# Late 1 / rms in both FFNs' first pairs, the second SSM group's gate and norm behind head 1, and whole first operands of out_proj, in a hybrid decoder layer

## The chip, the cores and the metric

The kernel runs on one core of one Trainium2 chip, as a single launch. The metric is device time in microseconds (us), taken as the median of several runs; lower is better. One execution was also recorded by the hardware profiler, and all rows of the trace come from it. The engines are named as in the profile: PE is the matrix engine (PEld its weight loads), DVE the vector engine, ACT the scalar engine, POOL GpSimd, SP the engine that issues nearly all DMAs.

## What is computed

One layer of a decoder that runs two mixers side by side, over 1048 tokens of width 1024: 16 learned meta tokens, 1024 prompt tokens and 8 single-token samples with states of their own.

```python
h = h + 0.5 * swiglu(rmsnorm(h, n1), w1g, w1u, w1d)      # first FFN, hidden width 2816
u = rmsnorm(h, nm) @ w_in
q, fz, iv, g, z, xbc, dt_raw = split(u)
# HGRN2, 4 heads of 128:  S_t = diag(f_t) S_{t-1} + k_t v_t^T,  o_t = S_t^T q_t
o_hg = rmsnorm_per_head(o_hg) * hg_norm * silu(g)
# Mamba-2, 8 heads of 64 in 2 groups, state 128, causal conv(4) on x/B/C
yz = y * silu(z)                                          # the gate
yz = yz * rsqrt(mean(yz * yz over the group) + EPS) * ssm_norm
h = h + concat([o_hg, yz]) @ w_out
h = h + 0.5 * swiglu(rmsnorm(h, n2), w2g, w2u, w2d)      # second FFN
y = rmsnorm(h, norm_final)

def swiglu(x, wg, wu, wd):
    return (silu(x @ wg) * (x @ wu)) @ wd
```

The states of both mixers after the prompt and after each sample are outputs too. All data are fp32.

## The kernel before

**Matmuls.** The activations lie transposed, features on the 128 partitions and 1048 tokens along the free axis, cut into four quarters of Q = 262 tokens. Every fp32 operand is split into a rounded high part (`cast`, `hi`; on ACT) and the difference that is left (`low`, `lo`; on DVE), and a product takes three matmuls, high x high, high x low, low x high (`mm3`, L143 to L145). All big products are bound by PE.

**FFN.** Gate and up together are one 2 x 2 block product, done by seven block products in place of eight (numbers 1 to 7). `Blocks` holds the seven operand blocks of one half of the tokens (o: half 0, e: half 1): `scaled` multiplies four tiles of h by the norm's weight column, `sum_` makes differences of blocks, `cast` and `low` split them. `Left` holds the seven weight blocks of one column pair. A *pair* is one column tile of gate and up, 14 *steps*: seven products for each of two halves, twelve matmuls a step. `Steps` is an order written by hand: functions hung up with `before(i, ...)` are issued ahead of step i's matmuls, the evacuation `post` behind them, and in the whole FFN each of PE, DVE, ACT and SP executes in this order (`manual_schedule`). 22 pairs follow each other, then `down`.

The activations are multiplied by the norm's weights before the product and by 1 / rms of the token behind it: `post` multiplies gate and up by `spread`, a tile that holds each token's 1 / rms on all partitions (`times_r`, L446), then applies Silu (L456, L464) and the product (L473). PSUM has four half banks for accumulation ("acc") and four small ones ("mis"), so a step can begin only when the evacuation of an earlier one is done.

Pair 0 of the first FFN also brings in the input: `first1` (L1637) loads ten token tiles, transposes them on PE (`place` L859, `place_k` L884), scales and copies them (L871, L875, L886, L887), squares them on ACT with a sum per token (`square`, L903), makes 1 / rms of each half (`rms`: `token_rstd` with a Sqrt, then five diagonal tiles, L918), and spreads it by matmuls of ones with the diagonal (`spread_r`, L924, L925). Its steps run half 0 through products 1, 2, 5, 6, 7, 3, then half 1, and then product 4 of both. Since product 2 and 3 are multiplied by 1 / rms in `post`, `post_first` keeps product 2 until 1 / rms of that half is there. Pair 0 of the second FFN (`first2`, L1810) has the same order with 1, 5, 2, 6, 7, 3, 4; there 1 / rms comes from `Norm` (squares on ACT, sums on POOL, a matmul of ones L211, `rstd` with Ln and Exp on ACT and three ops on DVE, L159 to L163), for the second half at step 2.

**Mixer.** Here a planner orders each engine's work by priority, which follows the order of the program, and by its own estimate of times; it may pull later work forward. `ssm_project` and `ssm_scan` come first, then the four HGRN heads: `hgrn_project` of q, f, v, `hgrn_scan` (L1383 to L1473, short matmuls between DVE ops of seven levels), `hgrn_project` of g, `hgrn_out` (norm and gate of the head). `ssm_gate` (two column tiles of z, 144 matmuls, Silu, product into y) and `ssm_norm` (squares on ACT, a sum on POOL L1261, matmuls of ones L1270, `rstd_wide`) are called for group 0 behind the scan of head 0, and for group 1 behind head 3. There `ssm_norm` stops after POOL's sum and hands the rest to `out_proj` as `mid`, which runs it ahead of its second block of weights.

**out_proj.** It adds two halves of the contraction to h, for two halves of the tokens: `opa` (heads 0 and 1, SSM group 0, which were spilled to memory in `md`) and `opb` (heads 2 and 3, group 1, `kept`). `opa` is loaded in three chunks of tokens and split into xhi and xlo, the tiles of the mixer's own input, when its last projection has read them. h is loaded from memory (`hsp`, L1781) into the eight "s" slots. There are 30 slots "u" and 8 slots "s" of 1056 columns, and nine temporaries "t".

Of the kernel before, what the change touches and what calls it, by code (L numbers as in the profile page):

```python
# [342 lines left out]
class Left:  # L343
# [84 lines left out]
def pair(K, S, wg, wu, f, ops, spread, hid, first=None):  # L428
# [6 lines left out]
    s0 = len(S.steps)  # L435
    tm = {}
# [12 lines left out]
    def post(p, cs, b):  # L449
        if p == 1:  # L450
            nc.scalar.copy(temp("z", cs), b)  # L451
        elif p == 6:
            nc.vector.tensor_add(temp("v", cs), b, temp("z", cs))
        elif p == 2:
# [6 lines left out]
        elif p == 3:  # L461
            nc.vector.tensor_add(temp("g1", cs), b, temp("v", cs))
            t = times_r("g1", 1, cs)
            nc.scalar.activation(t, t, AF.Silu)  # L464
            times_r("u1", 1, cs)
        else:
            nc.vector.tensor_add(temp("u0", cs), b, temp("v", cs))
            times_r("u0", 0, cs)
            if "h" not in tm:
                tm["h"] = True  # L470
                hid.append(K.slot("s", T))
            for n in range(2):
                nc.vector.tensor_mul(halves(hid[0][:, n * 2 * Q : n * 2 * Q + 2 * Q])[:, cs], temp(f"g{n}", cs), temp(f"u{n}", cs))  # L473

    if not first:
        left.plan(S, s0, int(f == 1))
# [5 lines left out]
    def post_first(p, cs, b):  # L482

        if p in (5, 2):
            late[p] = b
        elif p == 3:
            post(2, cs, late[2])
            post(3, cs, b)
# [202 lines left out]
def ffn(K, wg, wu, wd, ops, spread, src, first, after):  # L691
# [9 lines left out]
    with K.tc.manual_schedule(engines={E.PE, E.DVE, E.Activation, E.SP}):  # L701
        S = Steps()
        hidden = Hidden(K)
        for i in range(NF // 2):
            hid, e = [], []
            for f in (2 * i, 2 * i + 1):
                hid.append([])
                pair(K, S, wgv, wuv, f, ops, spread, hid[-1], first if f == 0 else None)
                e.append(len(S.steps))
            hidden.jobs(S, i, hid, *e)  # L710
# [113 lines left out]
class Input:  # L824
# [3 lines left out]
    def __init__(self, K, a, wcol, ops, spread):  # L828
# [3 lines left out]
        self.x, self.diag = {}, {}  # L832
# [72 lines left out]
    def store(self, half):  # L905
        dv = self.d.rearrange("(b k p) t -> b p k t", p=P, b=2)
        for q in (2 * half, 2 * half + 1):
            for b in range(2):
                self.K.nc.sync.dma_start(dv[b][:, :, q * Q : q * Q + Q], self.raw[b, q])

    def rms(self, half):

        K = self.K
        token_rstd(K, *(self.st[:, j, 5 * half : 5 * half + 5] for j in range(3)))
        d = self.diag[half] = K.t(2 * Q)
        for i in range(5):
            c = slice(P * i, min(P * i + P, 2 * Q))
            K.nc.scalar.activation(d[:, c], K.ident[:, : c.stop - c.start], AF.Identity, scale=self.st[:, 1, 5 * half + i : 5 * half + i + 1])  # L918

    def spread_r(self, half):  # L920
        K = self.K
        for n in range(2):
            ps = K.psm()[:, :Q]
            K.nc.tensor.matmul(ps, K.ones[1], self.diag[half][:, n * Q : n * Q + Q], start=True, stop=True)  # L924
            K.nc.scalar.copy(self.spread.quarter(2 * half + n), ps)  # L925
# [329 lines left out]
def ssm_norm(K, g, tag):  # L1255

    ya, yb = K.y[2 * g], K.y[2 * g + 1]
    v, r = K.slot(tag, w=T), K.slot(tag, w=T)
    K.nc.scalar.activation(v, ya, AF.Square)
    K.nc.scalar.activation(r, yb, AF.Square)  # L1260
    K.nc.gpsimd.tensor_add(v, v, r)  # L1261
    return lambda: ssm_norm_end(K, g, v, r)


def ssm_norm_end(K, g, v, r):
    nc = K.nc
# [247 lines left out]
def out_proj(K, a, h, part, ops, half, after=None, mid=None):  # L1514

    wv = a["w_out"][0].rearrange("(b s k p) c -> s p b k c", p=P, s=2, b=2)[part]
    for u in range(4):
        if u == 1 and mid:
            mid()
# [102 lines left out]
def body(ctx, tc, a, o):  # L1622
# [14 lines left out]
    def first1(S, w):  # L1637
# [33 lines left out]
        o.low(2)  # L1671
        o.sum_(5)
        w.lo(2)
        o.cast(5)
        w.sum_(5)
        w.hi(5)
        raw4(0)
        raw4(1)
        x.store(0)
        columns()  # L1680
        o.sum_(6)
        x.square(0)
# [7 lines left out]
        before(S, 1, (o.low, 5), (w.lo, 5), (o.cast, 6), (w.sum_, 6), (w.hi, 6), (o.sum_, 7), (x.square, 1))  # L1690
# [224 lines left out]
```

## Time and profile before

| what | us |
|---|---|
| runs, without the profiler | 2081.5, 2083.57, 2094.95 |
| median | 2083.57 |
| the profiled execution, its time | 2081.47 |
| its span, first to last instruction | 2079.8 |
| PE busy in it | 1970.9 |
| ACT busy from 30 to 60 us | 28.66 |
| PE busy from 30 to 60 us | 15.70 |

A row of the timeline reads: start, time taken, engine, line, operation, tile written <- tiles read, shape, how many in a row; in brackets the idle time of the engine before it and who ended it. A row of a table by stretch reads: stretch, its length, then busy time and number of instructions of PE, PEld, DVE, ACT and POOL, the mean clock that was granted to PE, the share of the DMA engines and their GB/s. Instructions of one engine overlap a little at their ends, so the distance from start to start is what one of them costs.

### The profile page before, as it was taken

The page shows a single profiled execution, that of the slowest core. Times are in us where ns is not written, and L with a number is a line of the kernel's source. Part 1 is how long each engine was busy: PE and PEld are TensorE (multiplying, and loading weights), DVE is VectorE, ACT ScalarE, POOL GpSimd, SP SyncE. Part 2 cuts the span into 40 slices and gives each one's busy share as a digit, 9 for nine tenths or more (in the row PEclk, how much of TensorE's full clock was granted, in tenths as well). Part 3 has the DMA queues.
Part 4 walks back from the last instruction along what each step waited for, and adds up shares of the span by engine and source line. Part 5 has one row for each costly group of instructions (what it writes and reads, how often), then busy time and mean ns, then how long its engine had stood idle before and what let it go on. Part 6 is the DMA issues. An engine that isn't in the chain of part 4 may idle for free.

```text
span 2079.8 us, 40798 instructions
## 1 busy us (share of the span) xinstructions
PE 1970.9 (95%) x16647; PEld 1915.7 (92%) x16647; DVE 1474.5 (71%) x2465; ACT 825.2 (40%) x1540; POOL 156.2 (8%) x197
## 2 busy tenths in 40 slices
PE   5899999999999899889989989989999999999996
PEld 5899999999999889888988878889999999999996
DVE  6777777777788676596455346777777777768973
ACT  7522222223534543574443344652222222354352
POOL 3000000000003210332011101210000000000000
PEclk8999999999999999999999999999999999999999
DMA  6223242335967621362022153222333242587851
GB/s 196 87 80 108 78 124 83 103 91 180 313 201 228 181 58 33 101 181 80 33 83 74 31 176 124 78 74 86 110 92 108 78 124 78 155 241 239 266 174 60
DMA packets 325042, 259.32 MB, mean 125 GB/s; under 512 B 17712, under 2 KB 301104, under 8 KB 324848
## 3 DMA queue, kind: packets, MB, share of 16 engines
q1 hardware_dynamic: 324616, 256.68, 40.7%
q8 instruction: 131, 2.15, 0.4%
q14 instruction: 55, 0.45, 0.1%
q0 software_dynamic: 224, 0.04, 0.0%
q10 hardware_dynamic: 16, 0.00, 0.0%
HBM read 191.26 MB, written 65.47 MB: 123 GB/s over the span
## 4 chain that ended last, share of the span: by engine, by line
PE 77%; DVE 10%; ACT 5%; DMA 4%; issue 3%; SPq 1%; POOL 0%; DVEq 0%; ACTq 0%; POOLq 0%
PE acc L143 24%; PE acc L145 23%; PE acc L144 23%; DMA r<-in_w_in_dram 1%; DVE u L561 1%; DVE ws L623 1%; DVE s L647 1%; DMA r<-in_w_ffn_up_dram 1%; DVE s L590 1%; DVE ws L138 1%; DMA r<-in_w_ffn_down_dram 1%; DVE u L287 0%; DVE ws L368 0%; PE mis L1449 0%; DVE r L613 0%
## 5 line engine op out<-in xcount | busy, mean ns | idle before, releaser
L143 PE MATMUL acc<-u,ws 128*128 128x262 f32 (+2 forms) x4504 | 1320.5, 294 | 39.3 <-ACT t L451 9.9
L145 PE MATMUL acc<-u,ws 128*128 128x262 f32 (+2 forms) x4504 | 1310.6, 291 | 0.6 <-DVE ws L368 0.5
L144 PE MATMUL acc<-u,ws 128*128 128x262 f32 (+2 forms) x4504 | 1309.1, 291 | 1.5 <-DVE u L561 1.5
L143 PEld LDWEIGHTS acc<-u,ws 128*128 128x128 f32 x4504 | 853.1, 190 | 54.4 <-ACT t L451 10.7
L144 PEld LDWEIGHTS acc<-u,ws 128*128 128x128 f32 x4504 | 857.8, 190 | 3.3 <-DVE u L561 1.9
L145 PEld LDWEIGHTS acc<-u,ws 128*128 128x128 f32 x4504 | 852.7, 189 | 2.6 <-DVE ws L368 1.1
L368 DVE TENSOR_TENSOR ws<-r,ws 128x512 fp32r<-128x512 f32 x308 | 211.7, 688 | 76.7 <-ACT ws L364 76.7
L364 ACT CAST ws<-r 128x512 fp32r<-128x512 f32 x308 | 173.2, 615 | 4.7 <-PE acc L145 3.1
L464 ACT ACTIVATE t<-t 128x524 f32<-128x524 f32 (+1 forms) x46 | 28.7, 623 | 305.4 <-DVE t L446 305.4
L360 DVE TENSOR_TENSOR r<-r,r 128x512 f32<-128x512 f32 x176 | 121.9, 695 | 11.7 <-DMA r<-in_w_ffn_up_dram 10.1
L204 POOL TENSOR_TENSOR t<-t,t 128x262 f32<-128x262 f32 x56 | 55.7, 1010 | 782.6 <-PE acc L145 626.6
L456 ACT ACTIVATE t<-t 128x524 f32<-128x524 f32 (+1 forms) x46 | 28.7, 624 | 215.3 <-DVE t L446 215.3
L561 DVE TENSOR_TENSOR u<-u,u 128x1048 fp32r<-128x1048 f32 (+1 forms) x84 | 97.8, 1166 | 8.8 <-ACT u L557 8.4
L138 DVE TENSOR_TENSOR ws<-r,ws 128x512 fp32r<-128x512 f32 x88 | 65.1, 753 | 48.0 <-ACT ws L137 47.9
L446 DVE TENSOR_TENSOR t<-t,u 128x524 f32<-128x524 f32 (+1 forms) x138 | 89.8, 679 | 3.3
L557 ACT CAST u<-u 128x1048 fp32r<-128x1048 f32 (+1 forms) x84 | 83.2, 993 | 1.3 <-DMA u<-hd 1.3
L647 DVE SCALAR_TENSOR_TENSOR s<-acc,s 128x524 f32<-128x524 f32 (+1 forms) x88 | 55.7, 648 | 38.1 <-PE acc L145 37.5
L137 ACT CAST ws<-r 128x512 fp32r<-128x512 f32 x88 | 53.9, 617 | 71.8 <-PE acc L145 42.4
L618 ACT CAST ws<-u 128x512 fp32r<-128x512 f32 (+1 forms) x72 | 42.1, 585 | 100.8 <-DVE u L613 95.0
L623 DVE TENSOR_TENSOR ws<-r,ws 128x512 fp32r<-128x512 f32 (+1 forms) x84 | 57.6, 697 | 32.6 <-ACT ws L618 32.5
L618 ACT CAST ws<-r 128x512 fp32r<-128x512 f32 (+1 forms) x84 | 47.4, 581 | 71.6 <-DVE r L613 41.0
L446 DVE TENSOR_TENSOR t<-acc,u 128x524 f32<-128x524 f32 (+1 forms) x46 | 31.3, 680 | 60.6 <-PE acc L145 60.6
(388 smaller groups left out, 1908.1 us busy)
## 6 DMA issues: line engine op xcount, KB each, us to landing
hd<-s SPq DMA_DIRECT2D x170, 262.0 KB
u<-hd SPq DMA_DIRECT2D x64, 524.0 KB
r<-in_w_ffn_down_dram SPq DMA_DIRECT2D x128, 256.0 KB
r<-in_w_ffn_gate_dram SPq DMA_DIRECT2D x88, 256.0 KB
r<-in_w_ffn_up_dram SPq DMA_DIRECT2D x88, 256.0 KB
r<-in_w_in_dram SPq DMA_DIRECT2D x56, 256.0 KB
r<-in_w_ffn_down_dram SPq DMA_DIRECT2D x64, 192.0 KB
u<-hd SPq DMA_DIRECT2D x28, 393.0 KB
```

The source lines that it names most:

```text
L138: self.nc.vector.tensor_sub(lo, src, hi.bitcast(F32))
L143: mm(ps, whi, xhi, start=first, stop=False, skip_group_check=more)
L144: mm(ps, whi, xlo, start=False, stop=False, skip_group_check=more)
L145: mm(ps, wlo, xhi, start=False, stop=last, skip_group_check=more)
L360: self.K.nc.vector.tensor_tensor(self.raw[p], self.raw[x], self.raw[y], op)
L364: self.K.nc.scalar.copy(self.w[p][:, : self.n * P], self.raw[p])
L368: self.K.nc.vector.tensor_sub(t[:, 512 : 512 + w], self.raw[p], t[:, :w].bitcast(F32))
L446: nc.vector.tensor_mul(t, t if src is None else src, spread.lanes(i, cs))
L557: K.nc.scalar.copy(hi, lo.bitcast(F32))
L561: K.nc.vector.tensor_sub(lo, lo.bitcast(F32), hi.bitcast(F32))
L618: nc.scalar.copy(w[p, j, g][:, : n * P], src)
L623: nc.vector.tensor_sub(t[:, 512 : 512 + n * P], box[0], t[:, : n * P].bitcast(F32))
```

## The change

It has three parts. What the layer computes stays the same; the multiplications by 1 / rms and the Silus of the first pairs are moved, not left out.

*First pairs.* In both FFNs pair 0's gate and up are evacuated without 1 / rms: product 2 is copied raw to `g0`, and `u0`, `g1`, `u1` are left as they are. Silu, the multiplications by 1 / rms and the two products are hung up at steps `late_r` to `late_r + 5`, for both halves at once, 524 columns wide: step 26 in the first FFN, 14 in the second. In the first FFN pair 1 keeps its product 2 raw too (`wait`), and applies Silu when product 3 is there. Squares move to steps 9 to 16 (that of the 12-token tile 4 to the beginning), one `rms` for all ten tiles stands at step 18 and `spread_r` of all quarters at step 22; the diagonals get a "u" slot. The order of casts, differences and transposes in `first1` is rewritten, with one `place_k` at most steps; the weight sums of pair 1 come three steps later. In the second FFN 1 / rms of the second half moves from step 2 to step 9.

*Mixer.* `ssm_gate` and `ssm_norm` of group 1 stand behind the scan of head 1, and the norm runs in one piece.

*out_proj.* `opa` gets eight slots of its own: each of its four tiles is loaded whole and split by one cast and one difference, behind the scan of head 3.

```diff
-    def plan(self, S, s0, late):
+    def plan(self, S, s0, late, sums):
-            ((5, 6, 7, 3), (-7, -7, -6, -5), self.sum_),
+            ((5, 6, 7, 3), [d + sums for d in (-7, -7, -6, -5)], self.sum_),
...
+    wait = late_r > 14
...
+        elif p == 2 and (f == 0 or wait and f == 1):
+            nc.scalar.copy(temp("g0", cs), b)
         elif p == 2:
             t = times_r("g0", 0, cs, b)
             nc.scalar.activation(t, t, AF.Silu)
...
         elif p == 3:
             nc.vector.tensor_add(temp("g1", cs), b, temp("v", cs))
-            t = times_r("g1", 1, cs)
-            nc.scalar.activation(t, t, AF.Silu)
+            if f == 0:
+                return
+            if wait and f == 1:
+                silu(0, cs)
+            silu(1, cs)
             times_r("u1", 1, cs)
         else:
             nc.vector.tensor_add(temp("u0", cs), b, temp("v", cs))
+            if f == 0:
+                return
             times_r("u0", 0, cs)
...
+    cs = slice(0, 2)
+    for i, (fn, *args) in enumerate(((silu, 0, cs), (silu, 1, cs), (times_r, "u0", 0, cs), (product_, 0, cs), (times_r, "u1", 1, cs), (product_, 1, cs))):
+        S.before(s0 + late_r + i, lambda fn=fn, args=args: fn(*args))
...
-            hidden.jobs(S, i, hid, *e)
+            hidden.jobs(S, i, hid, *([late_r + 6, max(late_r + 7, e[1])] if i == 0 else e))
...
-    def rms(self, half):
+    def rms(self):
         K = self.K
-        token_rstd(K, *(self.st[:, j, 5 * half : 5 * half + 5] for j in range(3)))
-        d = self.diag[half] = K.t(2 * Q)
...
+        token_rstd(K, *(self.st[:, j] for j in range(3)))
+        self.diag = K.slot("u", T)
+        for i, (t0, n) in enumerate(self.tiles):
+            K.nc.scalar.activation(self.diag[:, t0 : t0 + n], K.ident[:, :n], AF.Identity, scale=self.st[:, 1, i : i + 1])
...
      def first1(S, w):
...
-        before(S, 4, (o.low, 3), (w.lo, 3), (tail,), (e.cast, 1), (e.sum_, 5), (o.cast, 4), (x.place_k, 4), (x.rms, 0), (x.place_k, 5))
-        before(S, 5, (x.spread_r, 0), (o.low, 4), (e.cast, 5), (e.low, 1), (x.place_k, 6), (x.place_k, 7), (x.store, 1))
...
+        before(S, 5, (o.low, 3), (w.lo, 3), (e.cast, 1), (e.sum_, 5), (x.store, 1, (0,)), (x.place_k, 4), (x.place_k, 5))
+        before(S, 6, (e.low, 1), (e.cast, 5), (o.sum_, 4), (x.place_k, 6))
+        before(S, 7, (x.place_k, 7), (e.cast, 2), (e.low, 5), (e.low, 2), (e.sum_, 6), (x.store, 1, (1,)), (o.cast, 4))
...
+        before(S, 18, (x.rms,))
+        before(S, 22, *((x.spread_r, q) for q in range(4)))
...
-    ffn(K, a["w_ffn1_gate"][0], a["w_ffn1_up"][0], a["w_ffn1_down"][0], ops, spread, from1, first1, after1)
+    ffn(K, a["w_ffn1_gate"][0], a["w_ffn1_up"][0], a["w_ffn1_down"][0], ops, spread, from1, first1, after1, 26)
...
+    def split_spilled(i):
+        hi, lo = K.slot("u", T, F32R), K.slot("u", T, F32R)
+        nc.sync.dma_start(lo.bitcast(F32), md[i * P : (i + 1) * P, :])
+        nc.scalar.copy(hi, lo.bitcast(F32))
+        nc.vector.tensor_sub(lo, lo.bitcast(F32), hi.bitcast(F32))
+        return hi, lo
...
         pieces = hgrn_scan(K, a, o, hd, u)
+        if hd < 2:
+            ssm_gate(K, a, hd)
+            ssm_norm(K, hd, "s")
         if hd == 0:
-            ssm_gate(K, a, 0)
-            ssm_norm(K, 0, "s")()
             for i in range(2):
                 spill(2 + i, K.y[i])
+        if hd == 3:
+            opa = [split_spilled(i) for i in range(4)]
         u.update(hgrn_project(K, a, hd, "g"))
...
-    ssm_gate(K, a, 1)
     kept += K.y[2:]
-    opa = [(K.xhi[i], K.xlo[i]) for i in range(4)]
-    for c0, w in CHUNKS:
-        cs = slice(c0, c0 + w)
-        for i, (hi, lo) in enumerate(opa):
-            t = K.t(w)
-            nc.sync.dma_start(t, md[i * P : (i + 1) * P, cs])
-            K.split(t, hi[:, cs], lo[:, cs])
-    norm1 = ssm_norm(K, 1, "u")
...
-    out_proj(K, a, h, 0, opa, 0, mid=norm1)
+    out_proj(K, a, h, 0, opa, 0)
...
      def first2(S, w):
...
-        before(S, 2, (e.low, 2), (e.cast, 6), (e.sum_, 7), (nf2.end, 2), (nf2.end, 3, False))
-        before(S, 3, (e.low, 6), (e.cast, 7), (e.sum_, 4))
...
+        before(S, 8, (e.low, 3), (e.cast, 4))
+        before(S, 9, (nf2.end, 2), (nf2.end, 3, False), (w.hi, 4))
+        before(S, 10, (e.low, 4), (keep2, 1), (w.lo, 4))
...
-    ffn(K, a["w_ffn2_gate"][0], a["w_ffn2_up"][0], a["w_ffn2_down"][0], ops2, spread2, lambda o: hd2[o], first2, after3)
+    ffn(K, a["w_ffn2_gate"][0], a["w_ffn2_up"][0], a["w_ffn2_down"][0], ops2, spread2, lambda o: hd2[o], first2, after3, 14)
```

More of the change, by code (lines that the diff above doesn't have):

```diff
@@ L425, in halves, with pair @@
     return t.rearrange("p (c t) -> p c t", c=2)
-def pair(K, S, wg, wu, f, ops, spread, hid, first=None):
+def pair(K, S, wg, wu, f, ops, spread, hid, late_r, first=None):
     nc = K.nc
@@ L688, in down, with ffn @@
                         S.add(mm, (lambda p=p, j=j, c=c, box=box: post(p, j, slice(c, c + 1), box[0][:, None])) if g == 2 else None)
-def ffn(K, wg, wu, wd, ops, spread, src, first, after):
+def ffn(K, wg, wu, wd, ops, spread, src, first, after, late_r):
     NF = DFF // P
@@ L1508, in hgrn_out, with out_proj @@
     nc.vector.tensor_mul(g, g, r)
-def out_proj(K, a, h, part, ops, half, after=None, mid=None):
+def out_proj(K, a, h, part, ops, half, after=None):
     wv = a["w_out"][0].rearrange("(b s k p) c -> s p b k c", p=P, s=2, b=2)[part]
     for u in range(4):
-        if u == 1 and mid:
-            mid()
         wh, wl = K.weights(wv[:, :, :, u * 256 : (u + 1) * 256])
@@ L1670, in first1 @@
         raw3(1)
[L1671 to L1676, printed above, removed]
         raw4(0)
         raw4(1)
[L1679 to L1682, printed above, removed]
+        x.square(4)
+        o.low(2)
+        w.lo(2)
+        o.sum_(5)
         def tail():
```

80 lines of the change are left out of this document (40 added, 40 removed).

## The prediction

> **What bounds the kernel now.** I read the page first, then busy time by stretch, then the timeline of each engine where TensorE (PE) stands still, and last who released it.
>
> ```profile
> span 2079.8 us, 40798 instructions
> PE 1970.9 (95%) x16647; PEld 1915.7 (92%) x16647; DVE 1474.5 (71%) x2465; ACT 825.2 (40%) x1540; POOL 156.2 (8%) x197
> ```
>
> PE is idle for 2079.8 - 1970.9 = 109 us. The change takes no matmul away, so all that it can win is idle time of PE, and time in which PE runs at half clock. Stretches (the columns are PE, PEld, DVE, ACT, POOL busy, granted clock, DMA share, GB/s):
>
> ```profile
> 0.00:30.00 30.00, 19.05 (x112) 17.48 (x112) 21.80 (x37) 18.72 (x37) 18.76 (x52) 0.77 0.96 288
> 30.00:60.00 30.00, 15.70 (x86) 14.14 (x86) 19.55 (x31) 28.66 (x65) 0.00 (x0) 0.77 0.22 73
> 180.00:540.00 360.00, 358.96 (x2940) 358.49 (x2939) 268.05 (x408) 110.63 (x194) 0.00 (x0) 1.00 0.42 122
> 1240.00:1250.00 10.00, 5.30 (x31) 4.77 (x29) 6.27 (x8) 7.70 (x13) 2.40 (x1) 0.85 0.63 203
> 1250.00:1260.00 10.00, 9.60 (x56) 8.16 (x56) 6.95 (x18) 8.31 (x16) 0.00 (x0) 0.81 0.39 118
> 1370.00:1380.00 10.00, 3.63 (x22) 3.41 (x21) 8.54 (x14) 5.68 (x8) 0.00 (x0) 0.67 0.00 0
> 1380.00:1390.00 10.00, 9.44 (x63) 8.90 (x62) 7.10 (x13) 3.54 (x6) 0.00 (x0) 0.82 0.01 2
> ```
>
> From 180 to 540 PE is full: nothing in the middle of an FFN can be won, and a step of twelve matmuls costs 360 / 2940 x 12 = 1.47. The holes are the three places that the change touches: the opening of the first FFN (ACT has 28.66 of 30 from 30 to 60, so there ACT is the bound), the join between the mixer and out_proj near 1245, and the opening of the second FFN near 1375.
>
> **First FFN, what goes.** PE's first steps, and the queues that hold them up:
>
> ```profile
> 42.68 2.11 PE L924 MATMUL mis<-t,ones 128*128 128x262 f32 x4 [4.61 <-ACT t L918]
> 64.23 1.20 PE L924 MATMUL mis<-t,ones 128*128 128x262 f32 x4 [2.70 <-ACT t L918]
> ...
> 48.30 0.42 ACT L887 COPY u<-mis 128x250 f32<-128x250 f32 x1
> 48.74 1.28 ACT L456 ACT_TABLE_LOAD   x1
> 50.03 0.42 ACT L456 ACTIVATE t<-t 128x262 f32<-128x262 f32 x1
> ...
> 52.59 1.05 ACT L903 ACTIVATE s<-s 128x1024 f32<-128x1024 f32 x1
> ...
> 53.64 1.04 ACT L903 ACTIVATE s<-s 128x1024 f32<-128x1024 f32 x1
> ...
> 63.19 1.47 ACT L918 ACTIVATE t<-ident,st 128x128 f32<-128x128 f32 x5 [1.06 <-DVE st L945]
> ...
> 74.24 0.60 ACT L451 COPY t<-acc 128x524 f32<-128x524 f32 x1 [3.37 <-PE acc L145]
> ```
>
> The copy at 74.24 is that of pair 1's first product, two steps and a drain behind its start: pair 1 began at about 74.24 - 2 x 1.47 - 0.2 = 71.1. The change takes out of ACT's queue ahead of that point nine squares at 1.05 (52.59 to 53.64), 9.5; two sets of five diagonal tiles at 1.47, 2.9, with a 1.06 wait on DVE each, 2.1; three table loads at 1.28, 3.8; four copies of 1 / rms and four Silus, 262 wide, at no more than 0.42, 3.4. Together 21.7: ACT stops being the bound, and DVE becomes it. Prices on DVE:
>
> ```profile
> 53.04 1.24 DVE L287 TENSOR_TENSOR u<-u,u 128x1048 f32<-128x1048 f32 x1
> 54.20 1.24 DVE L298 TENSOR_TENSOR u<-u,u 128x1048 fp32r<-128x1048 f32 x1
> ...
> 48.55 0.78 DVE L446 TENSOR_TENSOR t<-t,u 128x262 f32<-128x262 f32 x2
> ...
> 86.70 1.28 DVE L368 TENSOR_TENSOR ws<-r,ws 128x512 fp32r<-128x512 f32 x2
> ...
> 93.74 1.32 DVE L473 TENSOR_TENSOR s<-t,t 128x524 f32<-128x524 f32 x2
> ```
>
> A difference 1048 wide takes 1.16 from start to start; of the pairs of rows that run back to back, half each: 512 wide 0.64, 524 wide 0.66, 262 wide 0.39. I lay the three queues end to end in the new order. The last of the eight transposed blocks leaves ACT at 48.7 now (the copy at 48.30). Ahead of it four squares (4.2), one diagonal set with its wait and sqrt (2.7) and two copies of 1 / rms (0.8) go, 7.7; the copy of the raw gate product and longer waits for DVE's sums give back 2.4 as I lay them, so it leaves at 43.4, and after one cast DVE can begin e.low(2) near 44.5. From there DVE has no hole up to w.lo(1) of pair 1: nine ops 1048 wide (10.4), six 512 wide (3.8), four 262 wide (1.6), 15.8, which ends at 60.3. Pair 1 begins at 60.3 in place of 71.1: **-10.8**, of which the end can take back:
> - the four ones-matmuls of spread_r lie in pair 1 now, where PE is full: 2 x 1.20, **+2.4**;
> - the six multiplications of pair 0 (two of Silu's inputs, two of up, two products), 524 wide, come at steps 26 to 31: 6 x 0.66 = 4.0 of DVE. A pair has 14 x 1.47 = 20.6 and DVE is busy 268 / 360 of it, so 5.2 are free, but not all in those six steps. Between 0 and 4.0 I take **+1.2**, nearer to nothing because the free time is there. ACT's squares at steps 10 to 16, one of 1.05 to a step of 1.47, are hidden by PE; without that cover they would cost what they save. rms at step 18 (ten diagonals, 2.9, and a sqrt between two trips to DVE, about 1.5) has the four steps to 22, 5.9, before spread_r and all of PE behind it wait for it;
> - PE still waits 1 to 4 at a time between the steps of pair 0. Such holes drop the clock (0.77 up to 60 is a mean of full and half clock), and steps at half clock cost 1.47 more each: between 0 and 3, I take **+1.5**.
>
> On SP the stores of the transposed input move by a step or two: behind them stand pair 1's four weight loads, whose sums move three steps later as well (to step 10), so I cost both at nothing; a late load would hold step 14 and all behind it. First FFN: -5.7, from -8.4 to -1.4.
>
> **Second FFN.**
>
> ```profile
> 1362.95 0.36 PE L143 MATMUL acc<-u,ws 128*128 128x262 f32 x1 [0.99 <-DVE s L1529]
> 1377.74 0.58 PE L143 MATMUL acc<-u,ws 128*128 128x262 f32 x1 [6.37 <-DVE t L458]
> ...
> 1369.44 1.28 ACT L153 ACT_TABLE_LOAD   x1
> ...
> 1374.06 0.43 DVE L163 SCALAR_TENSOR_TENSOR u<-t,t 128x262 f32<-128x262 f32 x1
> ...
> 1397.64 0.60 ACT L451 COPY t<-acc 128x524 f32<-128x524 f32 x1 [3.11 <-PE acc L145]
> ```
>
> Pair 0 begins at 1362.95, pair 1 at 1397.64 - 3.1 = 1394.5: 31.5 for 20.6 of steps. The chain of 1 / rms runs from the table load, 1369.44, to 1374.49, 5.05, and stands in DVE's queue ahead of the evacuation (L458) that PE waits for. The change puts the same chain at step 9. New order: nine steps 13.2, two waits of about 1 (z behind the casts, the bank of product 5), PE at 1378.2; the table load starts there, DVE is out of the chain at 1383.3, and the two ops 262 wide behind it (v, then x, which PE waits for) end at 1384.1, while PE has done the two ones-matmuls (1.2) and steps 9 and 10 (2.9) by 1382.3: what is late next is step 11, by 1.8. Then three steps (4.4) and about 1.2 on DVE's weights: pair 1 at 1389.7, **-4.8**. Against it: a hole of 2 can bring some half clock (now 0.67 and 0.82), 0 to 3.4, I take 1.7; the multiplications in pair 1, 0 to 4.0, I take 1.1. Second FFN: -2, from -4.8 to +2.6. [...]
>
> **Mixer.**
>
> ```profile
> 1246.54 2.40 POOL L1261 TENSOR_TENSOR u<-u,u 128x1048 f32<-128x1048 f32 x1 [48.26 <-ACT u L1260]
> 1247.45 2.60 DVE L138 TENSOR_TENSOR u<-u,u 128x1048 fp32r<-128x1048 f32 x1 [1.42 <-ACT u L137]
> 1248.99 1.53 PE L1270 MATMUL mis<-u,ones 128*128 128x350 f32 x2 [4.70 <-POOL u L1261]
> ...
> 1267.50 0.39 PE L143 MATMUL acc<-u,ws 128*128 128x262 f32 x1 [1.05 <-DVE s L1529]
> 1270.09 1.25 DVE L138 TENSOR_TENSOR u<-u,u 128x1048 fp32r<-128x1048 f32 x1
> ...
> L1261 POOL TENSOR_TENSOR s<-s,s x1: 2415/2415/2415, 981.0 to 981.0; 128x1048 f32<-128x1048 f32 x1
>   PE mis L1270: 4.7, 1
> ```
>
> The norm of group 1 now stands between the gate and out_proj with nothing under it: 4.70 idle. The clock falls there: 0.85 and 0.81 are 3.0 and 3.8 us at half rate, of which PE worked 4.8, so 2.4 lost. One wait of 1.05 on a DVE that is full of norm and splits goes too. The same norm of group 0, at 981 behind head 0, made no PE wait at all (line L1270 lists one wait, that of 1248.99). Behind head 1 it should be free: **-8.1**. With the gate go its four weight loads on SP, their casts and differences, and six Silus with six products, past the sample updates that POOL and SP do in scan 1. Its POOL add moves along: beside it a DVE difference took 2.60 instead of 1.25. In the old place that fell into the hole; in the new one it holds up the scan or hgrn_out of head 1: **+1.4**. [...]
>
> The scans change places as neighbours of the gate:
>
> ```profile
> 1047.36 0.81 PE L1407 MATMUL mis<-s,u 128*32 128x16 f32 x61 [1.25 <-DVE u L1422]
> 1194.44 2.71 DVE L138 TENSOR_TENSOR ws<-r,ws 128x512 fp32r<-128x512 f32 x2 [2.55 <-ACT ws L137]
> 1199.59 1.05 PE L1407 MATMUL mis<-s,u 128*32 128x16 f32 x64 [4.43 <-DVE u L1422]
> ...
> 1218.20 2.50 SPq L1781 DMA_DIRECT2D s<-hspill  x5
> ...
> 1231.24 1.24 DVE L1508 TENSOR_TENSOR u<-u,u 128x1048 f32<-128x1048 f32 x1
> ```
>
> Head 3, with the gate behind it, waited up to 4.43 at a level of the scan where head 1, without it, waited 1.25: the split of the gate's weights stood in DVE's queue. So the gate brings head 1 about what it takes from head 3: **0**, from -4 to +5. New is that head 3's end has only the g projection and out_proj's first half under it. That half doesn't need head 3, is 16 x 1.47 = 23.5 long, but each group ends in h, and the last five tiles of h are issued from 1218.20, at 128 x 1048 x 4 bytes and the 203 GB/s of the row above 2.6 each, so the last lands near 1234; head 3's result comes at 1232.5 and is split by 1235. PE has about as much work until then as it needs: between 0 and 5, I take **+2**. The operands of head 0, head 1 and group 0, whole: four loads and eight ops 1048 wide in place of twelve and twenty-four; they lie beside scan 3 and cost PE nothing unless they land late. Mixer: -4.7, from -12 to +3.
>
> **Sum.** -5.7 - 2 - 4.7 = -12.4. The profiled execution took 2081.47 with its launch, span 2079.8; the median of the three runs, 2083.57, is 2.1 above it. 2081.5 - 12.4 = 2069.1: I forecast 2069.
>
> **Rivals.**
> - *All of it arrives* (0.27): -8.4 in the first FFN, -4.8 in the second, -12.1 in the mixer: 2081.5 - 25.3 = 2056.2. For it: DVE has the free time. Against it: three places must work at once.
> - *The mixer gives its part back* (0.23): head 1's scan now waits for the gate's weights and the loads of the operands, +3 in the mixer instead of -4.7: 2077. For it: 4.43 at 1199.59. Against it: head 0 carried gate and norm.
> - *Head 3 stands bare* (0.10): slower. The gate, 144 matmuls 350 wide, no longer covers the loads. If the new operands get their slots only when scan 3 releases its own, twelve such tiles, 31.7, start where h's last five do now, near 1218, with 10 of other work for PE: a wait of 21.7, and about 3 of half clock behind it. With the norm's -8.1 and +1.4: 2081.5 - 7.7 - 6.7 + 24.7 = 2091.8. It decides from 14.4 upwards, and from 37 it is beyond 1%. Against it: h's first three tiles, and part of the eight new operands, find slots while scan 3 runs.
>
> The forecast's own case has 0.40.
>
> **Numbers.** 1% is 20.8, about what a measurement of this kernel can tell from no change: below 2062.7 is faster, above 2104.4 slower. The first rival nearly whole (0.25) and a thin edge of the forecast (0.04) are faster: 0.29. Of the last rival less than half (0.04) lies beyond 2104. The rest, 0.67, is within 1%. Range, 8 in 10: from the middle of the first rival, 2055, to the far side of the second, 2084.
>
> **What would show it.** Right: the copy of pair 1's first product between 63 and 65 instead of at 74.24, and PE's waits in pair 0 named by DVE's lows, not by L451; in the second FFN no wait of 6.37 but one near 2 at step 11; no PE wait at L1270; out_proj's first half starting straight behind scan 3. Wrong: a PE wait above 3 in scan 1, waits on s or on DMA in out_proj's first half, half clock through pair 0, or pair 2 longer than 21.

## The result, and the profile after

The changed kernel took 2063.53 us (median of 4 runs, 2059.26 to 2067.03) against 2085.03 for the kernel before beside it (4 runs, 2081.5 to 2094.95): ratio 0.9888, 95% interval 0.9847 to 0.993. The forecast was 2069, the range 2055 to 2084. The time lies inside, but the sum was little more than half of what the change gave: -12.4 forecast, -21.5 between the medians.

The page of the profiled execution after (2066.42 us with its launch), span and busy time by engine:

```profile
span 2064.7 us, 40746 instructions
PE 1980.8 (96%) x16647; PEld 1924.9 (93%) x16647; DVE 1469.8 (71%) x2439; ACT 824.6 (40%) x1530; POOL 158.4 (8%) x197
```

PE's idle time fell from 109 to 84, as the argument wanted. But PE was busy 10 us longer with the same 16647 instructions. That is, for the most part, half clock: 61.1 us of its busy time lay in stretches with a granted clock of 0.5, where the profile before had 43.1, and half of the difference is 9.0. This document comes back to it at its end. Stretches of the kernel after (the columns as in the prediction's table):

```profile
0.00:30.00 30.00, 21.23 (x115) 18.84 (x115) 21.25 (x37) 20.13 (x40) 20.37 (x52) 0.83 0.95 284
30.00:60.00 30.00, 22.95 (x140) 20.69 (x141) 24.89 (x33) 24.07 (x50) 0.00 (x0) 0.89 0.26 86
180.00:540.00 360.00, 358.34 (x2942) 357.90 (x2941) 267.56 (x409) 113.38 (x198) 0.00 (x0) 1.00 0.43 124
1235.00:1245.00 10.00, 10.00 (x74) 8.65 (x73) 4.93 (x13) 3.46 (x7) 0.00 (x0) 1.00 0.62 196
1360.00:1370.00 10.00, 6.85 (x52) 6.52 (x52) 6.64 (x11) 6.61 (x10) 0.00 (x0) 0.98 0.00 1
1370.00:1380.00 10.00, 9.30 (x55) 9.34 (x56) 8.57 (x16) 2.55 (x3) 0.00 (x0) 0.68 0.18 52
```

From 30 to 60 PE now works 22.95 instead of 15.70, at 0.89 of its clock instead of 0.77, and DVE (24.89) is ahead of ACT (24.07). Where the norm's hole was, at the join with out_proj, PE is full (10.00 from 1235 to 1245). The second FFN's opening still has a hole and a slow stretch. Rows of the timeline after, first FFN, then second:

```profile
41.60 0.38 ACT L903 COPY u<-mis 128x250 f32<-128x250 f32 x1
42.97 1.25 DVE L298 TENSOR_TENSOR u<-u,u 128x1048 fp32r<-128x1048 f32 x1 [2.19 <-ACT u L292]
58.87 0.29 PE L143 MATMUL acc<-u,ws 128*128 128x262 f32 x1
62.58 0.58 ACT L453 COPY t<-acc 128x524 f32<-128x524 f32 x1
71.11 1.93 PE L938 MATMUL mis<-u,ones 128*128 128x262 f32 x8
88.73 0.39 PE L145 MATMUL acc<-u,ws 128*128 128x262 f32 x1 [0.53 <-DVE ws L368]
...
1363.94 1.28 ACT L153 ACT_TABLE_LOAD   x1
1366.17 0.47 ACT L159 ACTIVATE t<-mis,eps 128x262 f32<-128x262 f32 x1
1367.83 0.52 ACT L160 ACTIVATE t<-t,lna 128x262 f32<-128x262 f32 x1 [1.19 <-DVE u L163]
1369.31 0.43 DVE L163 SCALAR_TENSOR_TENSOR u<-t,t 128x262 f32<-128x262 f32 x1
1370.12 0.43 DVE L462 TENSOR_TENSOR t<-acc,t 128x262 f32<-128x262 f32 x1
1370.70 0.56 PE L143 MATMUL acc<-u,ws 128*128 128x262 f32 x1 [3.84 <-DVE t L462]
```

The last transposed block leaves ACT at 42.0, pair 1 begins at 58.87 and its first product is copied at 62.58 instead of 74.24 (the prediction's sign was 63 to 65). In the second FFN the wait of 6.37 has become one of 3.84, behind a chain of 1 / rms that now starts at 1363.94.

Who released PE between scan 1 and out_proj's second quarter, kernel after (PE's line waits for a line: us in total, times, longest):

```profile
PE mis L1417 <- DVE u L1432: 4.9, 4, 1.8
PE mis L1417 <- DVE s L1434: 2.0, 1, 2.0
PE mis L1408 <- DVE u L1432: 1.9, 3, 0.9
PE mis L1280 <- POOL s L1276: 1.5, 1, 1.5
PE acc L143 <- DVE s L1537: 0.7, 4, 0.2
```

The norm's matmul of ones (L1280 now) waits 1.5 for POOL in place of 4.70. Of the others shown, the first three are the scans' own, and the last is out_proj's, for the additions into h.

### The profile page after: what moved, and what is told of

Read it like the earlier page. It is cut to its first block, busy times and chain, and to the rows that moved or that the text cites. A ratio compares the mean times of both kernels' runs of the same rounds, so it can differ in the third digit from the quotient of the medians.

```text
span 2064.7 us, 40746 instructions
## 1 busy us (share of the span) xinstructions
PE 1980.8 (96%) x16647; PEld 1924.9 (93%) x16647; DVE 1469.8 (71%) x2439; ACT 824.6 (40%) x1530; POOL 158.4 (8%) x197
## 4 chain that ended last, share of the span: by engine, by line
PE 75%; DVE 12%; ACT 4%; DMA 4%; issue 3%; SPq 0%; POOL 0%; DVEq 0%; ACTq 0%; POOLq 0%
PE acc L143 23%; PE acc L145 23%; PE acc L144 23%; DVE u L577 1%; DVE ws L639 1%; DMA r<-in_w_ffn_up_dram 1%; DVE s L663 1%; DVE u L629 1%; DMA s<-in_x_prompt_dram 1%; DVE u L298 1%; DMA r<-in_w_ffn_down_dram 1%; ACT ws L634 1%; PE mis L1154 1%; PE mis L1148 0%; DVE ws L368 0%
## 5 line engine op out<-in xcount | busy, mean ns | idle before, releaser
L143 PEld LDWEIGHTS acc<-u,ws 128*128 128x128 f32 x4504 | 856.1, 190 | 45.2 <-issue 12.5
L483 ACT ACTIVATE t<-t 128x524 f32<-128x524 f32 x47 | 30.3, 645 | 307.0 <-DVE t L448 307.0
L360 DVE TENSOR_TENSOR r<-r,r 128x512 f32<-128x512 f32 x176 | 122.1, 696 | 12.4 <-DMA r<-in_w_ffn_up_dram 10.7
L460 ACT ACTIVATE t<-t 128x524 f32<-128x524 f32 x41 | 26.4, 644 | 204.0 <-DVE t L448 204.0
L448 DVE TENSOR_TENSOR t<-t,u 128x524 f32<-128x524 f32 x135 | 90.9, 702 | 2.9
L453 ACT COPY t<-acc 128x524 f32<-128x524 f32 (+1 forms) x46 | 26.6, 579 | 106.2 <-PE acc L145 106.2
```

Source lines behind the costliest of these rows:

```text
L143: mm(ps, whi, xhi, start=first, stop=False, skip_group_check=more)
L360: self.K.nc.vector.tensor_tensor(self.raw[p], self.raw[x], self.raw[y], op)
L448: nc.vector.tensor_mul(t, t if src is None else src, spread.lanes(i, cs))
```

## The experiments

All programs have 16647 PE instructions, so the same matmul can be found in each by its number, wherever no part is moved past it. (In the new opening of the first FFN a transposition stands behind pair 0's first matmul instead of ahead of it, so there pair 0 begins one instruction earlier.) "FFN1 opening" is from the start of pair 0 to that of pair 4; "to ssm_project" from the end of the first FFN to ssm_project's first transposes, code that no kernel here changes; "heads" from the first matmul of scan 1 to out_proj's second quarter; "FFN2 opening" from the start of pair 0 to ten matmuls (1.2) into pair 4. Lengths are of the profiled execution, in us; times are medians, ratios against the kernel before on the same chip.

| kernel | FFN1 opening | to ssm_project | heads | FFN2 opening | us | ratio, 95% |
|---|---|---|---|---|---|---|
| before | 118.0 | 73.5 | 272.8 | 94.6 | 2085.03 | |
| after | 110.7 | 76.6 | 259.6 | 92.2 | 2063.53 | 0.9888, 0.9847 to 0.993 |
| after, again | 110.6 | 75.2 | 259.9 | 91.1 | 2062.08 | 0.9878, 0.9854 to 0.9902 |
| after, third | 110.1 | 76.7 | 263.9 | 92.3 | 2067.12 | 0.9885, 0.9864 to 0.9906 |
| first FFN alone | 110.5 | 76.5 | 275.1 | 94.7 | 2082.28 | 0.9963, 0.9948 to 0.9977 |
| mixer alone | 118.9 | 73.6 | 259.8 | 94.0 | 2079.54 | 0.9952, 0.9938 to 0.9967 |
| second FFN alone | 120.7 | 73.6 | 274.8 | 91.3 | 2086.35 | 0.9989, 0.9976 to 1.0003 |
| four squares early | 112.4 | 76.2 | 264.0 | 92.3 | 2066.54 | 0.9899, 0.9873 to 0.9926 |
| operands by chunk | 109.1 | 74.9 | 260.2 | 91.4 | 2062.72 | 0.9874, 0.9854 to 0.9893 |
| norm in out_proj | 110.1 | 74.9 | 266.0 | 91.4 | 2069.34 | 0.9902, 0.9882 to 0.9922 |
| gate behind head 2 | 110.8 | 73.6 | 264.9 | 91.2 | 2063.08 | 0.9876, 0.9857 to 0.9894 |
| late norm 2 | 111.0 | 77.7 | 262.9 | 88.4 | 2065.07 | 0.9878, 0.9859 to 0.9897 |
| late norm 2, POOL stores | 110.9 | 76.5 | 258.7 | 88.0 | 2061.13 | 0.9864, 0.9843 to 0.9885 |
| the same, again | 111.3 | 75.2 | 256.6 | 87.9 | 2056.27 | 0.9841, 0.982 to 0.9862 |

### Each part alone

The kernel before with one part of the change in each; the cuts from the diffs show a few lines of each part.

```diff
 # first FFN alone
-    ffn(K, a["w_ffn1_gate"][0], ..., from1, first1, after1)
+    ffn(K, a["w_ffn1_gate"][0], ..., from1, first1, after1, 26)
```

> The kernel before with the change of the first FFN alone. Theory (the two traces differ by 9.1 between the start of pair 0 and the start of pair 4, and by 9.5 at the end of the pairs): the part stands by itself; pair 1 starts near 59, pair 4 near 123.6 instead of 132.7, and the time is 9 us under the kernel before, give or take the 3 us by which half-clock windows of later code move. Rival (the prediction's own figure): the part is worth 5.7, and the rest of the 9.5 was luck of one execution; pair 4 then starts near 127.

Pair 4 started at 123.4 and the opening took 110.5, as in the change (110.7): the part stands by itself. The ratio is -0.37%, 7.7 of 2090. The opening is 7.5 shorter than the 118.0 of before, and 8.7 shorter than the mean of the three profiles with the old opening (119.2); the prediction had 5.7.

```diff
 # mixer alone
+        if hd < 2:
+            ssm_gate(K, a, hd)
+            ssm_norm(K, hd, "s")
...
+        if hd == 3:
+            opa = [split_spilled(i) for i in range(4)]
...
-    ssm_gate(K, a, 1)
```

> The kernel before with the change of the mixer alone (gate and norm of group 1 behind head 1, operands whole). Theory (between the first matmul of scan 1 and the start of out_proj's second quarter the changed kernel took 13.2 less): the part is worth 13, of which 11 fall into head 3 with out_proj's first half and 2 into heads 1 and 2; time 11 to 15 under the kernel before, no wait at the norm's matmul above 2. Rival (the prediction): 4.7, since head 1's scan takes over the wait of 4.43 that head 3 had.

The heads took 259.8, that is 13 under the 272.8 of before. The ratio is -0.48% or 10, just short of the 11 to 15 expected. By heads (scan to scan, the last to out_proj's second quarter) the lengths were 95.0, 73.4 and 91.4 where the kernel before had 72.3, 74.0 and 126.5.

```diff
 # second FFN alone
-        before(S, 2, (e.low, 2), (e.cast, 6), (e.sum_, 7), (nf2.end, 2), (nf2.end, 3, False))
+        before(S, 9, (nf2.end, 2), (nf2.end, 3, False), (w.hi, 4))
...
-    ffn(K, a["w_ffn2_gate"][0], ..., lambda o: hd2[o], first2, after3)
+    ffn(K, a["w_ffn2_gate"][0], ..., lambda o: hd2[o], first2, after3, 14)
```

> The kernel before with the change of the second FFN alone. Theory: the wait of 6.37 becomes one of 3.8 and a half-clock window of 3.4 goes with it, no more: 1.6 to 3 under the kernel before, within the noise of a median. Rival: the postponed multiplications fill DVE in pair 1 and give it back: 0 or slower, with waits of PE on the multiplications at L448 in pairs 1 and 2.

The opening took 91.3 for 94.6, with a wait of 3.87 at the known place; the interval of the ratio includes 1. The three ratios add up to -0.96%; the whole change gave -1.12 to -1.22%.

This kernel has the mixer of before, so its waits in head 1 are a second look at the same code. First head 1 of this kernel, then that of the kernel before:

```profile
PE mis L1500 <- DVE u L1515: 4.4, 1, 4.4
PE mis L1491 <- DVE u L1515: 1.0, 1, 1.0
...
PE mis L1407 <- DVE u L1422: 2.9, 2, 1.7
PE mis L1398 <- DVE u L1422: 1.6, 1, 1.6
```

The wait of 4.4 that the prediction saw in scan 3, and argued from, stands in scan 1 here, where the profile of before had none above 1.7 (the prediction's 1.25 was not its longest). So its place is that of one execution.

### First FFN: is ACT's queue what sets pair 1?

```diff
+        before(S, 1, ..., (columns,), (x.square, 0), (x.square, 1), (x.place_k, 0))
+        before(S, 2, ..., (w.hi, 6), (x.square, 2), (x.place_k, 1))
+        before(S, 3, ..., (w.hi, 7), (x.square, 3), (x.place_k, 2))
...
-        before(S, 10, (e.low, 3), (e.cast, 4), (w.hi, 4), (w.lo, 4), (x.square, 0), (x.square, 1))
+        before(S, 10, (e.low, 3), (e.cast, 4), (w.hi, 4), (w.lo, 4))
```

> The changed kernel with the squares of the first four tiles back in pair 0's first three steps, ahead of the transposed blocks' copies. Theory (ACT's queue up to the last transposed block is what sets pair 1's start, and DVE's chain of 15.8 follows it without a hole): four squares at 1.05 less the 1.5 of holes that ACT has there, the last copy at about 45 instead of 42.0, pair 1 near 61.8 instead of 58.9, pair 4 near 126.5 instead of 123.6, +3. Rival (PE's own waits on DVE set the pace, ACT has room): pair 1 near 59, 0.

Pair 1 came at 60.77 and pair 4 at 125.7, some 2 later than in the change. The last copy of a transposed block, a row of the timeline of this kernel:

```profile
42.78 0.38 ACT L903 COPY u<-mis 128x250 f32<-128x250 f32 x1
```

It ends at 43.2 instead of 42.0. So ACT's queue does still count, but the four squares (4.2) found about 3 of holes there, twice what I had counted: the size lies between the two theories.

### Mixer: the operands, the norm, the gate

```diff
-        if hd == 3:
-            opa = [split_spilled(i) for i in range(4)]
...
+    opa = [(K.xhi[i], K.xlo[i]) for i in range(4)]
+    for c0, w in CHUNKS:
...
+            nc.sync.dma_start(t, md[i * P : (i + 1) * P, cs])
+            K.split(t, hi[:, cs], lo[:, cs])
```

> The changed kernel with the operands of out_proj's first half as before (twelve loads by chunk, 24 operations, into the slots of the mixer's input, behind head 3), gate and norm staying behind head 1. Theory (the norm's hole is the gain, the operands cost nothing either way): scan 1 to out_proj's second quarter takes 259 to 262 as in the changed kernel. Rival: with the norm gone the chunks are what is late next, PE waits for them where it waited for the norm, 264 to 272.

The heads took 260.2, inside the 259.6 to 263.9 of the change's three profiles: the whole operands show neither gain nor cost by themselves.

```diff
         if hd < 2:
             ssm_gate(K, a, hd)
-            ssm_norm(K, hd, "s")
+        if hd == 0:
+            ssm_norm(K, 0, "s")()
...
+    norm1 = ssm_norm(K, 1, "u")
...
-    out_proj(K, a, h, 0, opa, 0)
+    out_proj(K, a, h, 0, opa, 0, mid=norm1)
```

> The changed kernel with the gate of group 1 behind head 1, but the end of its norm in the middle of out_proj's first half as before (one gate and operands as in the changed kernel). Theory (the hole of 4.70 is the chain gate, squares, POOL's sum, and the early gate alone breaks it): no wait at the norm's matmul, scan 1 to out_proj's second quarter 259 to 263. Rival (the norm itself has to leave out_proj: its table load, Ln, Exp and DVE operations stand between the splits of out_proj's weights): waits return there, 264 to 269.

The heads took 266.0, and a wait remains. A row of its timeline:

```profile
1248.89 3.72 PE L1284 MATMUL mis<-u,ones 128*128 128x350 f32 x6 [1.83 <-POOL u L1275]
```

The early gate cuts the hole from 4.70 to 1.83, but the norm in out_proj still costs: PE's idle time in head 3 and the join is 10.6 for 6.4 to 6.9 (table below). The theory that the gate alone does it has fallen. Against the means of the kernels with the old mixer, 274.2, and the new, 261.7, about 8 come with the gate and 4 with the norm. That is one profile, and about half of the 4 is half clock (13.6 us in the three heads, where the new mixer's six profiles have 9.6 in the mean).

```diff
-        if hd < 2:
-            ssm_gate(K, a, hd)
-            ssm_norm(K, hd, "s")
+        if hd in (0, 2):
+            ssm_gate(K, a, hd // 2)
+            ssm_norm(K, hd // 2, "s")
```

> The changed kernel with the gate and norm of group 1 behind head 2 instead of head 1. Theory (a scan that the gate covers does not have the next projections' weights in DVE's queue, so its waits go; head 1 was 3.8 shorter than before beyond the moved work): head 1 goes back to about 74.7 from scan to scan, head 2 becomes about 94.3, the sum of the three stretches stays within 1.5 of 260. Rival (the prediction's step: gate and scan bring one head what they take from another, 0): head 1's 3.8 was chance, the sum rises by 3 to 4.

The heads took 264.9, outside what the theory allowed. To read it, PE's idle time and the time at half clock by head (gaps between PE's records, and stretches with a granted clock of 0.5):

| kernel | head 1: idle, half | head 2 | head 3 and join |
|---|---|---|---|
| before | 5.3, 0 | 5.0, 3.4 | 14.5, 10.2 |
| first FFN alone | 6.2, 6.8 | 4.1, 3.4 | 11.8, 13.7 |
| second FFN alone | 5.5, 6.8 | 4.4, 3.4 | 14.0, 6.8 |
| after | 3.3, 0 | 4.5, 3.4 | 6.4, 3.4 |
| after, again | 3.3, 0 | 5.1, 3.4 | 6.9, 0 |
| gate behind head 2 | 5.3, 3.4 | 4.2, 3.4 | 5.5, 10.2 |
| norm in out_proj | 1.5, 0 | 4.5, 3.4 | 10.6, 10.2 |

Its idle time, 14.9, is that of the change (14.2 and 15.2); what made it 5 longer is 17 us at half clock for 7 and 3. The waits of its head 2:

```profile
PE mis L1417 <- issue: 2.7, 1, 2.7
PE mis L1280 <- POOL s L1276: 1.5, 1, 1.5
```

The scan's waits on DVE are gone there, as the theory said; in their place stood one of 2.7 that the profile names no releaser for. So a scan with the gate beside it does lose its waits on DVE, but this run can't settle what that is worth.

### Second FFN: the chain in pair 1

```diff
-        before(S, 9, (nf2.end, 2), (nf2.end, 3, False), (w.hi, 4))
+        before(S, 9, (w.hi, 4))
+        before(S, 17, (nf2.end, 2), (nf2.end, 3, False))
...
-    ffn(K, ..., first2, after3, 14)
+    ffn(K, ..., first2, after3, 26)
```

> The changed kernel, with the second FFN's 1 / rms moved once more: the two ends of the norm at step 17 (in pair 1) instead of step 9, and the multiplications at steps 26 to 31 as in the first FFN. Theory (the chain of 1 / rms in DVE's queue ahead of the evacuation is what PE waits 3.84 for in pair 0): that wait goes, and with it two half-clock windows, 3.4 to 6 us under the changed kernel, about 2058 to 2060. Rival: a full pair 1 has no room for the table load and the chain, PE waits there instead, 0 or slower than the changed kernel.

The waits of PE around the second FFN's opening in this kernel:

```profile
PE acc L143 <- DVE s L1537: 1.0, 1, 1.0
PE acc L143 <- ACT t L453: 1.0, 2, 0.6
PE acc L145 <- DVE ws L368: 0.7, 2, 0.6
```

The wait of 3.84 is gone and none came in pair 1; the opening fell to 88.4, 3.5 less than the mean of the change's three profiles. The median doesn't show it: 2065.07, where 2058 to 2060 was expected, and a ratio of 0.9878, as the change itself. Gains of this size drown in one set of five runs.

### The stores behind which SP stands

```diff
-        nc.sync.dma_start(o["hgrn_sample"][0, b0 : b0 + 4, hd].rearrange("b k v -> k b v"), sb)
+        nc.gpsimd.dma_start(o["hgrn_sample"][0, b0 : b0 + 4, hd].rearrange("b k v -> k b v"), sb)
```

(on top of the late norm). The reason was this stretch of the kernel before, in scan 1:

```profile
1045.23 0.38 SPq L1487 DMA_DIRECT2D out_dram<-r  x1
1046.03 0.55 SPq L125 DMA_DIRECT2D r<-in_w_in_dram  x1
...
1049.21 0.62 ACT L137 CAST ws<-r 128x512 fp32r<-128x512 f32 x1 [2.78 <-DMA r<-in_w_in_dram]
...
1047.14 3.22 DVE L138 TENSOR_TENSOR ws<-r,ws 128x512 fp32r<-128x512 f32 x2
...
1051.99 0.73 PE L1407 MATMUL mis<-s,u 128*32 128x16 f32 x64 [1.67 <-DVE u L1422]
```

SP issues the store at 1045.23, once POOL is done (its operation at L1483 ends at 1045.20), then a load of weights; ACT waits for it, and the differences of weights stand in DVE's queue in front of the scan's own operations, for which PE waits.

> The changed kernel with the late norm of the second FFN, and with the stores of the updated sample states issued on POOL's queue instead of SP's. Theory (in the scans SP stands at these stores until POOL has finished, the weight loads behind them land late, and their differences hold up the scan's operations in DVE's queue): the waits of 1 to 2.5 in scans 2 and 3 shrink, scan 1 to out_proj's second quarter falls from 260 to 254 to 257. Rival: the loads wait for buffers, not for the stores, and POOL's own issue costs more than it saves: 260 or more.

The heads took 258.7, above the 254 to 257 expected, and the median was 2061.13: head 3 with the join fell to 87.9 from 91.1, but head 1 had a wait of 2.12 and half clock, and took 98.4. On another chip, beside the change:

> The changed kernel, beside the next one on the same chip. Theory: 2060 to 2066, idle time of PE 70 to 75; its executions spread over 8 because half-clock windows fall by chance.

> The late norm of the second FFN and the sample stores on POOL's queue, once more. Theory: 3.5 less in the second FFN's opening and 1 to 3 less in head 3, so 3 to 6 under the changed kernel on the same chip. Rival: half-clock windows in other places take it, the two medians agree within 2.

The change took 2067.12, above the 2060 to 2066 expected, with 79 of idle time for 70 to 75 and executions that spread over 11.5. This kernel took 2056.27 beside it: more of a gain than expected, with a ratio of 0.9841 and an interval that ends at 0.9862, where the change's begins at 0.9864. The earlier pair (2061.13 and 2062.08) was apart by 1 only. Over all chips its nine executions have a median of 2059.6, the fourteen of the change 2065.2; the traces show some 7 (4 in the second FFN's opening, 3 in the heads). The 4 are the late norm's. For the stores the kernel to compare with is the late norm alone: its heads took 262.9 with 15.0 of idle time, against 258.7 and 256.6 with 13.0 and 11.2. But the change itself ran from 259.6 to 263.9 (14.2 to 16.0), and scan waits of up to 2.3 remained in both profiles, so how much of the 3 is the stores' and how much chance stays open. It is the fastest version that was run.

### The change once more

> The changed kernel itself, once more, to see which of its profile's holes and half-clock windows belong to it. Theory: the free-running windows of 3.41 decide which holes are paid twice; the opening of the first FFN (45.9 from pair 0 to pair 1), scan 1 to out_proj's second quarter (259.6) and the wait of 3.84 come again within 1, while the stretch from the end of the first FFN to scan 1 moves by several us. Rival: the 3 us lost behind the first FFN belong to the change; that stretch is 76.6 again.

The three stretches of the change came again within 1.2 (in the third profile the heads took 263.9, with 10 us at half clock in head 3 for 3.4 and none). The stretch behind the first FFN took 75.2, and in the gate-behind-head-2 kernel 73.6, as before the change. Its idle time was 6.0 to 6.5 in all fourteen profiles; its length is 73.5 to 73.6 where no half clock fell into it (four profiles), and up to 1.7 more for each window of 3.41 us at half clock, of which the others had one to three. So the 3 us are no work and no wait of the change. But ten of the eleven profiles with the new opening had such half clock there, and none of the three with the old; whether that is chance, three profiles can't tell.

## Why the prediction was right, and where it was off

**The base.** The sum was made against one execution of 2081.47. It is the fastest of 39 that were timed in the end; their medians on the other chips were 2089 to 2090. The change gave 23 to 25 by its three ratios. That the forecast lies only 5.5 above the result is in part luck: the base was 3.6 under the median beside the result, which made up for 3.6 of the 9.1 that the sum left out. By parts, what happened is near the rival "all of it arrives" (-25.3): -8.7 in the first FFN (mean of three profiles with the old opening, 119.2, against ten with the new, 110.5), -12.5 in the mixer (274.2 against 261.7, three and six profiles), -2.8 in the second FFN (94.4 against 91.6, three and eight), together -24.0.

**First FFN, -5.7 forecast.** The mechanism held: ACT stopped being the bound, and DVE's chain runs from the last block's e.low(2) to pair 1 with no hole above 0.6. Pair 1 began at 58.87 instead of 60.3: the chain began at 42.97 where I had 44.5, since ACT gave back less of the 7.7 than 2.4. From the start of pair 0 to that of pair 1 it took 45.9 for 56.5, 10.6 less where the sum had 10.8. The ones-matmuls cost 2.2 of the 2.4 (pair 1 took 22.8 for 20.6), the multiplications 1.1 of the 1.2 (pair 2 took 21.6 for 20.5, with a wait of 0.53 on a difference of weights behind them in DVE's queue). My mark "pair 2 longer than 21" was set too tight for a sum that held 1.2 for it. PE's waits in pair 0 were on DVE's lows as said, but for the longest, 2.43 on a cast of ACT (L292). The term that failed is the +1.5 of half clock: it was priced as if pair 0 kept its slow windows, while the filled holes took slow windows away (0.83 and 0.89 for 0.77 twice). No run shows its 1.47 more for a step at half clock either: in the profile of before twelve matmuls 0.219 apart instead of 0.122 make it 1.2 more. Without the term the sum is -7.2, and the two profiles give 7.3; the rest of the 8.7 is that the old opening's other two profiles were 1 and 3 longer.

**Mixer, -4.7 forecast.** Here the sum was wrong. The norm's hole went, as said, and its POOL sum left a wait of 1.5 (L1280) close to the +1.4, though on PE and not on DVE; the sign "no PE wait at L1270" did not hold. Two steps failed. "The scans exchange gate as neighbour, 0" rested on one wait of 4.43 in scan 3 that moves from scan to scan between executions; with the gate behind it head 1 has 3.3 of idle time in place of 5.3 to 6.2, POOL's 1.5 among it (why those waits went is open, see the gate behind head 2). And "+2 at the end of head 3" did not come: out_proj's first half follows scan 3 without a hole (10.00 of 10), and its waits on h sum to 0.7. The whole operands cost nothing, as said. Taken together, PE's idle time in the three heads fell from 23.6 to 15.0 (means of the three and the six profiles), and its time at half clock from 18.2 to 9.6, which is worth 4.3: the clock, for which the sum had 2.4, is a third of the gain.

**Second FFN, -2 forecast, -2.8 measured.** The step "late by 1.8" was 3.84. The chain began 15.9 behind pair 0's start (1348.03), where I had 15.2, and took 5.8 from the table load to the end of L163 where it took 5.05 before, since the second Exp (1367.83) waited 1.19 for the first quarter's DVE operations; PE was done with its own work 0.5 sooner than laid out. The evacuations of v and x stood behind, as said. Half clock came too: a window of 3.41 (1.7) in five of the eight profiles with the new opening, two windows in the other three, this one among them (0.68 from 1370 to 1380). The multiplications cost nothing where the sum had +1.1: pair 1 took 20.4 for the 20.8 of before. So the -2.8 lies near the -2 in part by luck: pair 0 gave 2.4 (31.4 against 29.0, means of three and eight) where the sum, half clock included, had 3.1, and pair 1 gave 0.4 instead of taking 1.1. The table load took 1.28, as before, and the activation behind it began 1.30 after the load's start, at 1365.24.

**The rivals.** Head 3 did not stand bare, and the mixer did not give its part back; what spoke for the latter was the one wait of 4.43.

## What to carry to other kernels

Work that isn't needed early (here 1 / rms, which can be applied behind the product) paid double here when it left the opening: its own time in ACT's queue, which was the bound (pair 1 came 10.6 sooner), and the slow clock of the stretch with the holes (0.89 from 30 to 60 instead of 0.77). Before arguing from a single wait, see whether it stands at the same place in a second profile of the same code; a wait that moves is worth its mean, not its size. Sum a forecast from the profiled execution, but set it against the median, or the luck of that execution enters the answer.

## What the runs showed of the hardware

In each of the fourteen profiles the stretches in which PE was granted half its clock begin on one grid of 3.41 us, to within 0.01, and the grid's offset from the first instruction was anything from 0.3 to 3.4 (1.17 in the profile of before, 0.90 in that of after). From 35.30 to 38.71 and from 42.13 to 45.54, for one, the profile of before has a clock of 0.50, and 1.00 in the windows beside them. I cut every profile into these windows (behind 70 us) and took PE's idle time in each from its records:

| idle in a window of 3.41 us | windows | at half clock in the next one |
|---|---|---|
| 1.9 and more | 79 | 79 |
| 1.7 to 1.9 | 26 | 16 |
| 1.0 to 1.7 | 203 | 14 |
| 0.5 to 1.0 | 343 | 12 |
| under 0.5 | 7481 | 31 |

With 1.9 or more of idle time in a window, the next was slow each time, 79 of 79; with less than 1.0, 43 times in 7824. Most of the 31 windows hold runs of small matmuls (16 rows, or 1 to 16 columns, in and around the scans), which count as busy in the records; why the clock fell behind them was not tested.

The same hole was followed by full clock in one profile and by half clock in another. Two stretches behind the first FFN, each beginning at a hole (2.53 and 2.35), in the kernel before:

```profile
702.80:708.80 6.00, 3.47 (x29) 3.45 (x29) 3.96 (x6) 1.53 (x4) 1.89 (x2) 1.00 0.81 227
722.90:728.90 6.00, 3.65 (x30) 3.56 (x30) 5.67 (x13) 3.56 (x9) 0.82 (x1) 1.00 0.75 221
```

and the same places in the kernel after (2.49 and 2.38):

```profile
693.20:699.20 6.00, 3.51 (x21) 3.42 (x21) 4.00 (x6) 1.57 (x4) 1.92 (x3) 0.83 0.70 205
714.90:720.90 6.00, 3.62 (x18) 3.54 (x18) 5.02 (x12) 2.66 (x7) 0.81 (x1) 0.73 0.75 221
```

Before, the grid cut the first hole into 1.49 and 1.04, and PE did 29 matmuls behind it at full clock; after, 1.98 of it fell into one window, and PE did 21 at 0.83. Three profiles of the one changed program had 65, 41 and 58 us at half clock with 72, 74 and 79 of idle time (both between PE's first and last matmul), and took 2066.4, 2059.2 and 2070.5. What half clock costs is a little less than half: in the profiles of before and after, matmuls of 262 columns begin every 0.219 us at half clock and every 0.122 at full clock. With half of what fell into such stretches taken off, PE's busy time is 1949 to 1955 in all fourteen profiles, while as the page gives it it runs from 1970.5 to 1981.9. Idle time and half clock together make the spread of this kernel, and a change of 3 us can't be told by a few runs, only by its stretch of the trace.
